# Delta-net stage of a two-layer trunk: a shorter key-norm chain, the first value pairs convolved from a copy, the inverse's placement rewritten

## The chip, the cores and the metric

The kernel runs on one core of a Trainium2 chip. A core has a matrix engine (PE, with its weight loads shown apart as PEld), and three elementwise engines: VectorE (DVE), ScalarE (ACT) and GpSimd (POOL). SyncE (SP) issues the DMAs. Each engine has its own queue of instructions, written out when the program is built, and waits in it on semaphores. The metric is device microseconds of one execution; lower is better. All times below are us unless another unit stands beside them.

## The reference

The input is one sequence of 256 tokens of width 1024. Two layers each add a half-weighted feed-forward block, a mixer and another half-weighted feed-forward block, each with an RMS norm ahead of it and behind it. The mixer of layer 0 is a gated short convolution. That of layer 1, where the change lies, is a gated delta rule:

```python
proj = x @ w_in                                  # q, k, v, z, b, a
qkv = silu(causal_depthwise_conv(qkv, conv_w))   # width 4
q, k = l2norm(q), l2norm(k)                      # 8 heads of 128, each used by 2 of 16 value heads
a = where(strict, (k_beta @ k.T) * decay, 0)     # per head and chunk of 64 tokens
t_inv = triangular_solve(eye + a, eye)
u, w = t_inv @ v_beta, t_inv @ (k_beta * exp(g))
# scan over chunks: v_new = u - w S; o = q_g S + qk v_new; S = S exp(g_last) + k_tail^T v_new
o = o * rsqrt(mean(o*o) + eps) * norm_w * silu(z)
out = o @ w_out
```

All of it is in float32.

## The kernel before

The 256 tokens are kept in SBUF. Tokens come in two tiles of 128 (index t, NT = 2). The weights are streamed: each piece of 512 KB is loaded to a buffer `raw` (3 buffers), split by ScalarE into a rounded part `whi` (L119) and by VectorE into the remainder `wlo` (L121); both have 8 buffers. Each product is then three matmuls, activation-high by weight-high, activation-low by weight-high and activation-high by weight-low. Most of the program is such products, back to back on PE.

The delta-net mixer (`gdn_proj`) issues its work in this order. Two head slabs give the gates and the first key and query heads. The tiles a0, a1, a2 (`stat_group`, L278 to L280, 24 matmuls of 256 columns for each head's part) give the other keys and queries; each is convolved (`conv`: one ScalarE instruction L584 and three on VectorE, L586) and passed through silu (L573). Three z groups follow, z0, z1 and z2 (`act_group`, L221, L222, L225: 24 matmuls of 512 columns for each of the two token tiles), then four value groups v0 to v3 (`stat_group` again, two pairs each), then z3, then the output product.

Beside these run chains that wait for their turn. `kq_chain` takes four groups of two key heads: PE transposes a head (L618) and forms the products of keys with keys and with queries (L621) in PSUM banks named `acc`; ScalarE copies the transposed key (`ktok`, L624) and part of the head (L625), and sums squares with four activations L630 into `kss`; POOL adds a small constant to all eight sums (L634), VectorE takes the reciprocal (L636), POOL multiplies it into `dsc` (L639), VectorE scales the products into `KQ` (L645, eight instructions), and ScalarE copies the eight 32-row diagonal blocks to `Ld` (L652). When all four groups are there, `invert` starts: VectorE transposes `Ld` (L669), then runs 31 steps of two dependent instructions (L677 multiplies, L679 subtracts) on all diagonal blocks at once, and transposes the result twice, to `Xd` (L681) and `Yd` (L683). POOL copies `Yd` into KQ. PE then forms products of 32 x 32 blocks in two halves: L707, whose `blk` operand is `Xd`, L718 and L719, and so on. `v_pair` convolves a pair of value heads straight from the PSUM bank, applies silu, transposes on PE (L757) and scales on ScalarE (L759). `scan` needs the inverse and the values.

Two things set the order. In the program, each chain is a generator that a ticker resumes: every few matmuls of a group are a tick, and `yield n` waits n ticks; INV_WAIT is the wait between the inverse's transposes and its products, V_WAIT that between a value pair's silu and its transposes. A scheduler then writes each engine's queue from this program by its own estimate of when operands are ready, so an instruction can stand earlier or later in the queue than in the program. Once built, a queue's order is fixed.

Of the kernel before, what the change touches and what calls it, by code (L numbers as in the profile page):

```python
# [7 lines left out]
F32 = mybir.dt.float32  # L8
F32R = mybir.dt.float32r
AF = mybir.ActivationFunctionType  # L10
ALU = mybir.AluOpType
PSUM = bass.MemoryType.PSUM

P = 128
T = 256
NT = 2
# [5 lines left out]
NG = 4  # L22
B32 = 32
EPS = 1e-6
# [6 lines left out]
NBIG = 8  # L31
NROW = 3
KQ_WAIT = 3
INV_WAIT = 37
V_WAIT = 4
SCAN_WAIT = 2
ORD = "00111222"
GORD = "00012222"
# [11 lines left out]
def trunk_kernel(ctx: ExitStack, tc: tile.TileContext, x, norm_g, w_gu, w_dn, sc_in, sc_cw, sc_out,  # L50
                 gdn_h0, gdn_h1, gdn_a0, gdn_a1, gdn_a2, gdn_v, gdn_z, gdn_cw, gdn_al, gdn_dt, gdn_nw, gdn_out, eye, upper, slower, out, stop=None):
    nc = tc.nc
    V, S, G, PE = nc.vector, nc.scalar, nc.gpsimd, nc.tensor
# [6 lines left out]
    sp = ctx.enter_context(tc.tile_pool(name="sp", bufs=2))  # L60
# [16 lines left out]
    phalf = const.tile([P, 4], F32, name="phalf")  # L77
# [49 lines left out]
    def slab(shape, dtype, name):  # L127
        return hp.tile(shape, dtype, name=name, tag="slab")
# [347 lines left out]
    def gdn_proj(xh, xl, mid):  # L476
# [102 lines left out]
        KQ = [[None] * NT for _ in range(NG)]  # L579
# [25 lines left out]
        def kq_chain():  # L605

            for gi in range(NG):
                ss = sp.tile([P, NT, 2, 2], F32, name="kss", bufs=2)
                k1 = slab([P, 2, 2, P], F32, "kq1")
                pkq = []  # L610
                for i in range(2):
                    kh = 2 * gi + i
                    while kq[kh] is None or tk.now < kq_time[kh] + KQ_WAIT:
                        yield 1
                    tp = side_bank().rearrange("p (t c) d -> p t c d", t=NT)
                    for t in range(NT):
                        for c in range(2):
                            PE.transpose(tp[:, t, c, :], kq[kh][:, c, t * P:(t + 1) * P], ident)  # L618
                    pk = side_bank().rearrange("p (t c) d -> p t c d", t=NT)
                    for t in range(NT):  # L620
                        PE.matmul(pk[:, t, :, :], lhsT=kq[kh][:, 0, t * P:(t + 1) * P],  # L621
                                  rhs=kq[kh][:, :, t * P:(t + 1) * P], start=True, stop=True)
                    pkq.append(pk)
                    S.activation(ktok[:, kh, :], tp[:, 0, 0, :], AF.Copy)  # L624
                    S.activation(k1[:, i, :, :], kq[kh][:, :, P:], AF.Copy)  # L625
                    kq1[kh] = k1[:, i, :, :]
                    for t in range(NT):
                        for c in range(2):
                            junk = sp.tile([P, 512], mybir.dt.bfloat16, name="junk", bufs=1)
                            S.activation(junk[:, 0:P], tp[:, t, c, :], AF.Square, accum_out=ss[:, t, c, i:i + 1])  # L630
                    yield 1
                while dec[1][gi] is None:
                    yield 1
                G.tensor_scalar(ss, ss, EPS, None, ALU.add)  # L634
                rk = sp.tile([P, NT, 2], F32, name="rk", bufs=2)
                V.reciprocal(rk, ss[:, :, 0, :])  # L636
                dd = small(f"dsc{gi}", 8).rearrange("p (t n) -> p t n", t=NT)
                for t in range(NT):
                    G.tensor_tensor(dd[:, t, :].rearrange("p (k v) -> p k v", k=2),  # L639
                                    beta[:, t, 4 * gi:4 * gi + 4].rearrange("p (k v) -> p k v", k=2),  # L640
                                    rk[:, t, :].unsqueeze(2).broadcast_to([P, 2, 2]), ALU.mult)
                for t in range(NT):
                    m = big([P, 4, 2, P], F32, "KQ")
                    for hv in range(4):
                        V.scalar_tensor_tensor(m[:, hv, :, :], pkq[hv // 2][:, t, :, :], dd[:, t, hv:hv + 1],  # L645
                                               bc(dec[t][gi][:, hv, :], 2), ALU.mult, ALU.mult)
                    KQ[gi][t] = m
                    for b in range(4):
                        r = slice(b * B32, (b + 1) * B32)
                        o = Ld[r, :, 8 * gi + t:8 * gi + t + 7:2].rearrange("p i v -> p v i")  # L650
                        i_ = m[r, :, 0, b * B32:(b + 1) * B32]
                        S.activation(o, i_, AF.Copy)  # L652
                n = small(f"nk{gi}", 4).rearrange("p (t n) -> p t n", t=NT)
                G.tensor_tensor(n, ss[:, :, 0, :], phalf.rearrange("p (t n) -> p t n", t=NT), ALU.pow)
                q = small(f"eq{gi}", 4).rearrange("p (t n) -> p t n", t=NT)
                G.tensor_scalar(q, ss[:, :, 1, :], 128.0 * EPS, None, ALU.mult)
                w = small(f"wt{gi}", 4)
                G.tensor_tensor(w, etail[:, 4 * gi:4 * gi + 4], dd[:, 0, :], ALU.mult)
                Dsc[gi], nk[gi], eq[gi], wt[gi] = dd, n, q, w
                yield 1  # L660
            tk.start(invert())


# [3 lines left out]
        def invert():  # L667
# [5 lines left out]
            for j in range(B32 - 1):  # L673
                n, m = B32 - 1 - j, j + 1
# [5 lines left out]
            Xd = row("blk").rearrange("p (a b) -> p a b", a=B32)  # L680
# [1 line left out]
            Yd = row("blk").rearrange("p (a b) -> p a b", a=B32)  # L682
            V.transpose(Yd.rearrange("p h i -> p i h"), X)  # L683
            T1 = row("blk").rearrange("p (a b) -> p a b", a=B32)
            for gi in range(NG):
                for t in range(NT):
                    for b in range(4):
                        r = slice(b * B32, (b + 1) * B32)
                        G.tensor_copy(KQ[gi][t][r, :, 0, r], Yd[r, 8 * gi + t:8 * gi + t + 7:2, :])
            yield INV_WAIT  # L690
            for half in range(2):
                hs = slice(16 * half, 16 * half + 16)
                gis = (2 * half, 2 * half + 1)
                E = {}
                for gi in gis:
                    E[gi] = slab([P, 8, 64], F32, "E64")
                    for b in range(2):
                        r = slice(b * B32, (b + 1) * B32)
                        G.tensor_copy(E[gi][r, :, r], Xd[r, 8 * gi:8 * gi + 8, :])
                    G.memset(E[gi][0:B32, :, B32:], 0.0)  # L700
                pt = side_bank().rearrange("p a (b c) -> p (a b) c", c=B32)
                for x in range(16):
                    ht = 16 * half + x
# [42 lines left out]
        nv = [None] * NG  # L746

        def v_pair(gi, i, pt, tiles):
            vc = sp.tile([P, 2, T], F32, name="yb")
            for j in range(2):  # L750
                conv(vc[:, j, :], pt[:, j, :], 16 + 4 * gi + 2 * i + j)
            silu(vc, vc)
            yield V_WAIT
            tp = ps.tile([P, NT, 2, P], F32, name="mm")
            for t in range(NT):
                for j in range(2):
                    PE.transpose(tp[:, t, j, :], vc[:, j, t * P:(t + 1) * P], ident)  # L757
            for t in range(NT):
                S.activation(tiles[t][:, 2 * i:2 * i + 2, :], tp[:, t, :, :], AF.Copy,  # L759
                             scale=nk[gi][:, t, i:i + 1])  # L760
            if i == 1:
                nv[gi] = tiles
# [293 lines left out]
```

## Time and profile before

| what | value |
|---|---|
| median of 3 runs | 1127.42 us (1125.82 to 1130.31) |
| profiled execution, own time | 1128.42 us |
| its span | 1126.5 us |
| mean granted PE clock | 0.995 |
| PE busy | 1100.2 us, 98% of the span |
| DVE, ACT, POOL busy | 749.9, 651.8, 88.8 us |
| HBM read | 195.99 MB |

The span is the time from the first to the last instruction of the profiled execution. PE's share is so high because nearly all of the program is matmuls in a row; where PE idles, it does so for single waits of a fraction of a microsecond to some microseconds. The delta-net stage lies at about 660 to 925 us of the span. In a timeline row, the number in square brackets is the engine's idle time ahead of the instruction and the instruction that ended it; the column after the start is the duration of the whole row.

### The profile page before, as it was taken

Reading aid. Unit: us, or ns where it says so; the run is one execution under the profiler, and the core shown is the slowest. Engines: PE = TensorE matmul, PEld = TensorE weight load, DVE = VectorE, ACT = ScalarE, POOL = GpSimd, SP = SyncE. Lnnn points to the kernel's source line nnn. Section 1 sums busy time; section 2 is a strip of 40 time slices with the busy share of each in tenths; the row PEclk is TensorE's granted clock in tenths of the full one; section 3 lists DMA queues with packets and bytes.
Section 4 is the critical chain, followed back from the end, with each engine's and each line's share of the span. In section 5 each row is a group of like instructions: output and inputs, shape, how many; then the busy total and the mean of one; then the engine's idle time right before and its main releaser. Section 6 shows DMA issues by size and latency. Waiting matters only on the chain.

```text
span 1126.5 us, 16842 instructions
## 1 busy us (share of the span) xinstructions
PE 1100.2 (98%) x6284; PEld 942.4 (84%) x6284; DVE 749.9 (67%) x1140; ACT 651.8 (58%) x1201; POOL 88.8 (8%) x167
## 2 busy tenths in 40 slices
PE   9999999999999999999999999889899999999997
PEld 6888887888788888788888877778899887888886
DVE  7776735687777663577765468768946557767543
ACT  6666535545556653556664358784587645666432
POOL 0100000000200000010000012110141212000000
PEclk9999999999999999999999999999999999999999
DMA  8755555656566565576555653327332355655552
GB/s 271 244 185 190 191 166 167 225 180 198 182 223 204 171 206 165 163 229 209 189 185 169 193 185 113 94 94 227 114 129 76 131 168 168 213 199 190 185 168 75
DMA packets 55955, 198.12 MB, mean 176 GB/s; under 512 B 6721, under 2 KB 7233, under 8 KB 55874
## 3 DMA queue, kind: packets, MB, share of 16 engines
q1 hardware_dynamic: 55728, 196.99, 54.2%
q8 instruction: 49, 0.80, 0.3%
q14 instruction: 32, 0.26, 0.1%
q10 hardware_dynamic: 146, 0.07, 0.0%
HBM read 195.99 MB, written 1.05 MB: 175 GB/s over the span
## 4 chain that ended last, share of the span: by engine, by line
PE 81%; DVE 7%; ACT 5%; DMA 3%; issue 2%; POOL 2%; SPq 0%; DVEq 0%; POOLq 0%; ACTq 0%
PE mm L298 27%; PE mm L301 14%; PE acc L324 7%; PE acc L325 7%; PE acc L323 7%; PE mm L221 3%; PE mm L222 3%; PE mm L225 3%; DVE wlo L121 2%; ACT whi L119 1%; ACT blk L652 1%; DVE kq L586 1%; PE mm L176 1%; ACT junk L147 1%; DMA raw<-in_w_gu 1%
## 5 line engine op out<-in xcount | busy, mean ns | idle before, releaser
L121 DVE TENSOR_TENSOR wlo<-raw,whi 128x1024 fp32r<-128x1024 f32 (+2 forms) x362 | 437.5, 1220 | 240.2 <-ACT whi L119 201.5
L119 ACT ACTIVATE whi<-raw 128x1024 fp32r<-128x1024 f32 (+2 forms) x362 | 376.1, 1051 | 224.3 <-PE acc L325 104.6
L298 PE MATMUL mm<-x,whi 128*128 128x512 f32 x1312 | 329.4, 393 | 0.0
L298 PEld LDWEIGHTS mm<-x,whi 128*128 128x128 f32 x1312 | 235.9, 189 | 42.4
L301 PEld LDWEIGHTS mm<-x,wlo 128*128 128x128 f32 x1312 | 179.0, 190 | 12.8
L301 PE MATMUL mm<-x,wlo 128*128 128x256 f32 x1312 | 182.9, 282 | 0.0
L323 PE MATMUL acc<-whi,hb 128*128 128x512 f32 x352 | 136.5, 388 | 0.0
L324 PE MATMUL acc<-wlo,hb 128*128 128x512 f32 x352 | 135.6, 385 | 0.3 <-DVE wlo L121 0.3
L325 PE MATMUL acc<-whi,hb 128*128 128x512 f32 x352 | 135.3, 385 | 0.0
L308 ACT ACTIVATE corr<-mm 128x256 f32<-128x256 f32 x164 | 61.2, 376 | 67.4 <-PE mm L301 65.6
L221 PE MATMUL mm<-whi,x 128*128 128x512 f32 (+1 forms) x240 | 94.4, 394 | 0.9 <-ACT x L178 0.7
L222 PE MATMUL mm<-wlo,x 128*128 128x512 f32 (+1 forms) x240 | 94.2, 393 | 0.7 <-DVE wlo L121 0.7
L225 PE MATMUL mm<-whi,x 128*128 128x512 f32 (+1 forms) x240 | 87.8, 389 | 0.2 <-DVE x L179 0.2
L324 PEld LDWEIGHTS acc<-wlo,hb 128*128 128x128 f32 x352 | 66.2, 188 | 13.8 <-DVE wlo L121 0.8
L323 PEld LDWEIGHTS acc<-whi,hb 128*128 128x128 f32 x352 | 66.2, 188 | 13.1
L325 PEld LDWEIGHTS acc<-whi,hb 128*128 128x128 f32 x352 | 66.1, 188 | 13.2
L154 POOL TENSOR_SCALAR rstd<-ss 128x1 f32<-128x1 f32 x24 | 12.3, 513 | 786.1 <-ACT junk L147 786.1
L278 PE MATMUL mm<-x,whi 128*128 128x256 f32 x200 | 59.7, 299 | 2.0 <-DVE kq L586 2.0
L279 PE MATMUL mm<-x,whi 128*128 128x256 f32 x200 | 58.4, 292 | 0.0
L280 PE MATMUL mm<-x,wlo 128*128 128x256 f32 x200 | 57.9, 289 | 0.0
L222 PEld LDWEIGHTS mm<-wlo,x 128*128 128x128 f32 x240 | 45.2, 188 | 11.2 <-DVE wlo L121 2.9
L221 PEld LDWEIGHTS mm<-whi,x 128*128 128x128 f32 x240 | 45.2, 188 | 11.1 <-ACT x L178 2.7
(216 smaller groups left out, 1238.3 us busy)
## 6 DMA issues: line engine op xcount, KB each, us to landing
raw<-in_w_gu SPq DMA_DIRECT2D x176, 512.0 KB, 4.2
raw<-in_w_dn SPq DMA_DIRECT2D x88, 512.0 KB, 3.6
raw<-in_sc_in SPq DMA_DIRECT2D x24, 512.0 KB, 4.1
raw<-in_gdn_z SPq DMA_DIRECT2D x16, 512.0 KB, 3.9
raw<-in_gdn_v SPq DMA_DIRECT2D x16, 512.0 KB, 4.2
raw<-in_gdn_out SPq DMA_DIRECT2D x16, 512.0 KB, 3.7
gamma<-in_norm_g SPq DMA_DIRECT2D x11, 512.0 KB, 5.4
raw<-in_gdn_a SPq DMA_DIRECT2D x9, 512.0 KB, 4.4
```

The costliest lines, as they stand in the source:

```text
L119: S.activation(hi[:, r], raw[:, r], AF.Copy)
L121: newest[0] = V.tensor_tensor(lo[:, r], raw[:, r], hi[:, r], ALU.subtract).ins
L221: PE.matmul(pt, lhsT=xh[:, t, k, :], rhs=hi, start=(k == 0), stop=False)
L222: PE.matmul(pt, lhsT=xh[:, t, k, :], rhs=lo, start=False, stop=False)
L225: PE.matmul(pt, lhsT=xl[:, t, j, :], rhs=part(j)[0], start=False, stop=(j == KD - 1))
L278: PE.matmul(ptile, lhsT=hi, rhs=h2, start=(k == 0), stop=False)
L298: PE.matmul(flat, lhsT=part(k, 0), rhs=xx[:, k].rearrange("p h t q -> p (h t q)"), start=(k == 0), stop=False)
L301: PE.matmul(flat[:, T:], lhsT=part(k, 1), rhs=xx[:, k, 0].rearrange("p t q -> p (t q)"), start=False, stop=(k == KD - 1))
L308: S.activation(c, pt[:, 1, :], AF.Copy)
L323: PE.matmul(o, lhsT=yh(c, t), rhs=hi[:, r], start=(c == 0), stop=False)
L324: PE.matmul(o, lhsT=yh(c, t), rhs=lo[:, r], start=False, stop=False)
L325: i = PE.matmul(o, lhsT=yl(c, t), rhs=hi[:, r], start=False, stop=(c == n - 1)).ins
```

## The change

In the key-norm chain, `kss` is laid out with the keys' sums first. The squares come ahead of the copies of `ktok` and of the head, and the key's two ahead of the query's two. The addition of the constant and the two `dsc` products go from POOL to VectorE, the addition for the four key sums alone; POOL adds the constant for the queries' sums where it scales them. Of the eight block copies of a group (four for each token tile), the four of rows 64 to 127 go from ScalarE to POOL. In `invert`, the fills of `E` and the copies of the diagonal blocks are written as a function, called for the first half of the heads ahead of the wait and for the second half behind it, with POOL's order fixed among them; the wait is 41 ticks where it was 37. In `v_pair`, the pairs of v0 and v1 are first copied by ScalarE from their PSUM bank to a slab buffer `vraw` and convolved from there; the wait ahead of their transposes is 8 ticks where it was 4, and 4 for v2 and v3 as before. Behind the change the lines of `gdn_proj` have other numbers: L618 becomes L619, L645 L646, L669 L673, L677 and L679 become L681 and L683, L681 and L683 become L685 and L687, L707 becomes L724, L711 L728, L757 L778.

```diff
-INV_WAIT = 37
-V_WAIT = 4
+INV_WAIT = 41
+V_WAIT = (8, 8, 4, 4)
+VRAW = 2
...
-                ss = sp.tile([P, NT, 2, 2], F32, name="kss", bufs=2)
+                ss = sp.tile([P, 2, NT, 2], F32, name="kss", bufs=2)
...
+                    for c in range(2):
+                        for t in range(NT):
+                            junk = sp.tile([P, 512], mybir.dt.bfloat16, name="junk", bufs=1)
+                            S.activation(junk[:, 0:P], tp[:, t, c, :], AF.Square, accum_out=ss[:, c, t, i:i + 1])
                     S.activation(ktok[:, kh, :], tp[:, 0, 0, :], AF.Copy)
                     S.activation(k1[:, i, :, :], kq[kh][:, :, P:], AF.Copy)
                     kq1[kh] = k1[:, i, :, :]
-                    for t in range(NT):
-                        for c in range(2):
-                            junk = sp.tile([P, 512], mybir.dt.bfloat16, name="junk", bufs=1)
-                            S.activation(junk[:, 0:P], tp[:, t, c, :], AF.Square, accum_out=ss[:, t, c, i:i + 1])
...
-                G.tensor_scalar(ss, ss, EPS, None, ALU.add)
+                V.tensor_scalar(ss[:, 0], ss[:, 0], EPS, None, ALU.add)
                 rk = sp.tile([P, NT, 2], F32, name="rk", bufs=2)
-                V.reciprocal(rk, ss[:, :, 0, :])
+                V.reciprocal(rk, ss[:, 0])
                 dd = small(f"dsc{gi}", 8).rearrange("p (t n) -> p t n", t=NT)
                 for t in range(NT):
-                    G.tensor_tensor(dd[:, t, :].rearrange("p (k v) -> p k v", k=2),
+                    V.tensor_tensor(dd[:, t, :].rearrange("p (k v) -> p k v", k=2),
...
-                        S.activation(o, i_, AF.Copy)
+                        if b < 2:
+                            S.activation(o, i_, AF.Copy)
+                        else:
+                            G.tensor_copy(o, i_)
...
+            E, placed = {}, [None]
+
+            def place(half):
+
+                gis = (2 * half, 2 * half + 1)
+                for gi in gis:
+                    E[gi] = slab([P, 8, 64], F32, "E64")
+                    for b in range(2):
+                        r = slice(b * B32, (b + 1) * B32)
+                        with tc.issue_after(placed[0]) if placed[0] else nullcontext():
+                            G.tensor_copy(E[gi][r, :, r], Xd[r, 8 * gi:8 * gi + 8, :])
+                    with tc.issue_after(placed[0]) if placed[0] else nullcontext():
+                        last = G.memset(E[gi][0:B32, :, B32:], 0.0).ins
+                placed[0] = last
...
+            place(0)
             yield INV_WAIT
             for half in range(2):
...
+                if half:
+                    place(1)
                 pt = side_bank().rearrange("p a (b c) -> p (a b) c", c=B32)
...
+            if gi < VRAW:
+                raw = slab([P, 2, T], F32, "vraw")
+                S.activation(raw, pt, AF.Copy)
+                pt = raw
...
-            yield V_WAIT
+            yield V_WAIT[gi]
```

What this does to the queues is seen at three places. The first is PE's queue around the inverse's first products (`blk` is Xd; a number behind a name tells buffers apart). Before, they stand among the matmuls of v2's first pair (bank 7875), behind the transposes of three value pairs:

```order
L757 MATMUL mm_7888<-ident_81,yb_7803 128x128 x2
...
L280 MATMUL mm_7875<-x2_5783,wlo_7852 128x256
L278 MATMUL mm_7875<-x2_5783,whi_7857 128x256
L279 MATMUL mm_7875<-x2_5783,whi_7857 128x256
L280 MATMUL mm_7875<-x2_5783,wlo_7858 128x256
L707 MATMUL acc_7937<-blk_7350,KQ_6831 32x32
L707 MATMUL acc_7937<-blk_7350,KQ_6840 32x32 x2
```

After the change they stand between z2's first token tile (bank 7495) and its second (bank 7522), ahead of every value group (v0's first bank is 7575):

```order
L223 MATMUL mm_7495<-wlo_7492,x2_5783 128x512
L226 MATMUL mm_7495<-whi_7491,x2_5783 128x512
L724 MATMUL acc_7988<-blk_7350,KQ_6831 32x32
L724 MATMUL acc_7988<-blk_7350,KQ_6840 32x32 x2
...
L222 MATMUL mm_7522<-whi_7473,x2_5783 128x512
L223 MATMUL mm_7522<-wlo_7474,x2_5783 128x512
...
L279 MATMUL mm_7575<-x2_5783,whi_7551 128x256
```

So the products moved ahead past z2's second tile, all of v0 and v1 and a part of v2's first pair. The second place is VectorE's queue in the steps of the inverse. Before, convolutions (L586) and weight remainders (L121) stand among the steps up to the last one:

```order
L677 TENSOR_TENSOR sg<-blk 128x247
L586 SCALAR_TENSOR_TENSOR yb<-mm,gcw,yb 128x255
L679 TENSOR_TENSOR blk<-blk,sg 128x13x19
L586 SCALAR_TENSOR_TENSOR yb<-mm,gcw,yb 128x254
L677 TENSOR_TENSOR sg<-blk 128x240
L586 SCALAR_TENSOR_TENSOR yb<-mm,gcw,yb 128x253
L679 TENSOR_TENSOR blk<-blk,sg 128x12x20
```

After the change the last weight remainder (L122) among them is that of v0's fourth piece; from the subtraction over 22 x 10 on, 43 instructions of the steps follow in a row up to the two transposes, and v1's remainders and the first convolutions (now L587, from `vraw`) come behind:

```order
L681 TENSOR_TENSOR sg<-blk 128x220
L122 TENSOR_TENSOR wlo<-raw,whi 128x1024
L683 TENSOR_TENSOR blk<-blk,sg 128x22x10
L681 TENSOR_TENSOR sg<-blk 128x231
...
L683 TENSOR_TENSOR blk<-blk,sg 128x31
L685 STREAM_TRANSPOSE blk<-blk 128x32x32
L687 STREAM_TRANSPOSE blk<-blk 128x32x32
L122 TENSOR_TENSOR wlo<-raw,whi 128x1024 x4
L587 SCALAR_TENSOR_TENSOR yb<-vraw,gcw,yb 128x255 x2
```

The third place is VectorE's queue at the last key-norm group. Before:

```order
L121 TENSOR_TENSOR wlo<-raw,whi 128x1024 x3
L636 RECIPROCAL rk<-kss 128x4
L645 SCALAR_TENSOR_TENSOR KQ<-acc,dsc_7210,dec 128x256 x8
L121 TENSOR_TENSOR wlo<-raw,whi 128x1024
L669 STREAM_TRANSPOSE blk<-blk 128x1024
```

After:

```order
L122 TENSOR_TENSOR wlo<-raw,whi 128x1024 x2
L635 TENSOR_SCALAR kss<-kss 128x4
L122 TENSOR_TENSOR wlo<-raw,whi 128x1024
L637 RECIPROCAL rk<-kss 128x4
L640 TENSOR_TENSOR dsc_7210<-beta,rk 128x4 x2
L646 SCALAR_TENSOR_TENSOR KQ<-acc,dsc_7210,dec 128x256 x8
L122 TENSOR_TENSOR wlo<-raw,whi 128x1024
L673 STREAM_TRANSPOSE blk<-blk 128x1024
```

The addition and the two products are now in VectorE's own queue, in front of the eight scalings.

More of the change, by code (lines that the diff above doesn't have):

```diff
@@ L651, in kq_chain @@
                         i_ = m[r, :, 0, b * B32:(b + 1) * B32]
-                        S.activation(o, i_, AF.Copy)
+                        if b < 2:
+                            S.activation(o, i_, AF.Copy)
+                        else:
+                            G.tensor_copy(o, i_)
                 n = small(f"nk{gi}", 4).rearrange("p (t n) -> p t n", t=NT)
-                G.tensor_tensor(n, ss[:, :, 0, :], phalf.rearrange("p (t n) -> p t n", t=NT), ALU.pow)
+                G.tensor_tensor(n, ss[:, 0], phalf.rearrange("p (t n) -> p t n", t=NT), ALU.pow)
                 q = small(f"eq{gi}", 4).rearrange("p (t n) -> p t n", t=NT)
-                G.tensor_scalar(q, ss[:, :, 1, :], 128.0 * EPS, None, ALU.mult)
+                G.tensor_scalar(q, ss[:, 1], EPS, 128.0 * EPS, ALU.add, ALU.mult)
                 w = small(f"wt{gi}", 4)
@@ L684, in invert @@
             T1 = row("blk").rearrange("p (a b) -> p a b", a=B32)
-            for gi in range(NG):
-                for t in range(NT):
-                    for b in range(4):
-                        r = slice(b * B32, (b + 1) * B32)
-                        G.tensor_copy(KQ[gi][t][r, :, 0, r], Yd[r, 8 * gi + t:8 * gi + t + 7:2, :])
+            E, placed = {}, [None]
[4 more added lines that the diff above has]
+                    for b in range(2):
+                        r = slice(b * B32, (b + 1) * B32)
+                        with tc.issue_after(placed[0]) if placed[0] else nullcontext():
[3 more added lines that the diff above has]
+                placed[0] = last
+                for gi in gis:
+                    for t in range(NT):
+                        for b in range(4):
+                            r = slice(b * B32, (b + 1) * B32)
+                            with tc.issue_after(placed[0]):
+                                last = G.tensor_copy(KQ[gi][t][r, :, 0, r], Yd[r, 8 * gi + t:8 * gi + t + 7:2, :]).ins
+                placed[0] = last
+            place(0)
             yield INV_WAIT
@@ L693, in invert @@
                 gis = (2 * half, 2 * half + 1)
[L694 to L700, printed above, removed]
+                if half:
+                    place(1)
                 pt = side_bank().rearrange("p a (b c) -> p (a b) c", c=B32)
```

## The prediction

> **What bounds the kernel now.** I read the page's busy times first, then PE's waits in the delta-net stage, then the timelines around each wait. The page:
>
> ```profile
> PE 1100.2 (98%) x6284; PEld 942.4 (84%) x6284; DVE 749.9 (67%) x1140; ACT 651.8 (58%) x1201; POOL 88.8 (8%) x167
> ```
>
> PE is the bound nearly everywhere, so an edit on another engine is worth what it takes away from, or adds to, PE's idle time. All the change's instructions lie in the delta-net stage. PE's waits there, 640 to 940 us (us in total, times, longest):
>
> ```profile
> PE acc L618 <- ACT kq L573: 3.6, 2, 3.1
> PE mm L757 <- ACT yb L573: 3.4, 1, 3.4
> PE mm L278 <- DVE kq L586: 2.0, 1, 2.0
> PE acc L621 <- DVE KQ L645: 1.7, 1, 1.7
> PE acc L718 <- ACT blk L711: 0.4, 1, 0.4
> PE acc L707 <- DVE blk L681: 0.2, 1, 0.2
> ```
>
> These six make 11.3 us, most of what any reordering here could win. The last row matters: the inverse's first products wait 0.2 us for Xd, so before the change they stand at just the right place. PE's timeline gives each wait's place and what follows it:
>
> ```profile
> 732.18 1.13 PE L621 MATMUL acc<-kq 128*128 128x256 f32 x4 [1.71 <-DVE KQ L645]
> 746.69 1.12 PE L618 MATMUL acc<-ident,kq 128*128 128x128 f32 x4 [3.06 <-ACT kq L573]
> 750.09 0.39 PE L221 MATMUL mm<-whi,x 128*128 128x512 f32 x1
> 767.13 0.39 PE L221 MATMUL mm<-whi,x 128*128 128x512 f32 x1
> 772.57 0.39 PE L221 MATMUL mm<-whi,x 128*128 128x512 f32 x1
> 778.01 0.28 PE L278 MATMUL mm<-x,whi 128*128 128x256 f32 x1
> 794.53 1.12 PE L757 MATMUL mm<-ident,yb 128*128 128x128 f32 x4 [3.41 <-ACT yb L573]
> 795.65 0.41 PE L279 MATMUL mm<-x,whi 128*128 128x256 f32 x1
> 797.57 0.37 PE L279 MATMUL mm<-x,whi 128*128 128x256 f32 x1
> 797.90 0.28 PE L278 MATMUL mm<-x,whi 128*128 128x256 f32 x1
> 798.02 0.28 PE L279 MATMUL mm<-x,whi 128*128 128x256 f32 x1
> ```
>
> z1's second tile ends at 767.13, z2's first runs from there to 772.57 (5.44 us), z2's second to 778.01. Behind the 3.41 us wait the clock is low: nine steps take 797.57 - 795.65 = 1.92 us, 0.213 each, where one takes 0.12 (797.90 to 798.02). With the four transposes this loses 1.5 us. Behind the 3.06 us wait the same count (746.69 to 750.09 is 3.40 us for about 1.4 us of work at full clock) gives 2.0 us. The granted clock in the slices of 10 us (start:end, length, PE, PEld, DVE, ACT, POOL, then the clock) agrees:
>
> ```profile
> 740.00:750.00 10.00, 6.94 (x26) 5.48 (x25) 6.08 (x11) 8.55 (x30) 0.25 (x2) 0.83 0.36 110
> 790.00:800.00 10.00, 6.59 (x44) 6.39 (x43) 9.97 (x26) 6.57 (x10) 0.00 (x0) 0.83 0.22 63
> ```
>
> A page of the Trainium skill, "TensorE: Matmul & The Clock Gate" (Part 1, What's actually happening), says the clock is halved after an idle window of about 3.4 us; by it every wait of that length costs some 1.7 us more (an estimate: half of one such window), as the two slices of this trace show. The sum stands on the 1.5 and 2.0.
>
> **The key-norm part: a gain of 6.5 us on PE.** The last group's chain across ACT, POOL and DVE:
>
> ```profile
> 744.43 1.04 ACT L119 ACTIVATE whi<-raw 128x1024 fp32r<-128x1024 f32 x1
> 746.02 0.62 ACT L573 ACTIVATE kq<-kq 128x512 f32<-128x512 f32 x1
> 748.81 0.28 ACT L630 ACTIVATE junk<-acc 128x128 bf16<-128x128 f32 x1
> 749.67 0.24 POOL L634 TENSOR_SCALAR kss<-kss 128x8 f32<-128x8 f32 x1 [12.43 <-ACT junk L630]
> 749.94 0.18 DVE L636 RECIPROCAL rk<-kss 128x4 f32<-128x4 f32 x1 [2.43 <-POOL kss L634]
> 751.65 3.23 DVE L645 SCALAR_TENSOR_TENSOR KQ<-acc,dsc,dec 128x256 f32<-128x256 f32 x8 [1.53 <-POOL dsc L639]
> 753.34 1.85 ACT L652 ACTIVATE blk<-KQ 32x128 f32<-32x128 f32 x4 [0.82 <-DVE KQ L645]
> 756.18 1.80 ACT L652 ACTIVATE blk<-KQ 32x128 f32<-32x128 f32 x4
> 758.02 1.25 DVE L669 STREAM_TRANSPOSE blk<-blk 128x1024 f32<-128x1024 f32 x1 [2.01 <-ACT blk L652]
> ```
>
> From the sums' end (749.67) to the first scaling (751.65) the chain takes 2.0 us through POOL and back. In VectorE's queue the addition, the reciprocal and two products are four small instructions, 0.1 to 0.2 each by the 0.18 row, with one weight remainder between them: 1.6, so 0.4 won in the last group and 1.4 in one with no remainder between. The key's squares are done two squares (0.8) sooner. Half the block copies leave ACT: 1.85 becomes 0.9, while POOL, 8% busy, does the rest in the same time. ACT so frees about 0.9 per tile ahead of each silu and weight split, and the silu at 746.02 that PE waited for comes some 3 us earlier. Following each queue in its new order from 707 us on with durations from such rows, I get the last group's sums at 744.7 (before 749.6) and the chain's transpose at 751.1 (before 758.0). On PE the waits of 3.06 and 1.71 and the 2.0 of low clock go, 6.8, and a little is given back where a product waits for the copy of `ktok`, which now stands behind four squares: 0.3. So z1 ends at 767.13 - 6.5 = 760.6, z2's first tile at 766.0. Bounds: nothing (the VectorE queue now holds what POOL did, and a late square would stop its remainders and convolutions too), and 7.3, all of the four rows' L618 and L621 waits with the clock, without L278's 2.0, whose predecessors are the same.
>
> **The moved products: the term that decides.** PE's queue now holds the first products between z2's two tiles. They need Xd, and VectorE's queue holds ahead of Xd eight weight remainders, among them v0's four, and the whole chain:
>
> ```profile
> 760.40 1.21 DVE L121 TENSOR_TENSOR wlo<-raw,whi 128x1024 fp32r<-128x1024 f32 x1
> 761.53 0.20 DVE L679 TENSOR_TENSOR blk<-blk,sg 128x31 f32<-128x31 f32 x1
> 773.68 0.39 DVE L679 TENSOR_TENSOR blk<-blk,sg 128x220 f32<-128x220 f32 x1
> 788.07 0.42 DVE L677 TENSOR_TENSOR sg<-blk 128x252 f32<-128x252 f32 x1
> 788.53 0.42 DVE L679 TENSOR_TENSOR blk<-blk,sg 128x252 f32<-128x252 f32 x1
> 809.80 2.20 DVE L681 STREAM_TRANSPOSE blk<-blk 128x1024 f32<-128x1024 f32 x1
> 811.89 1.96 DVE L683 STREAM_TRANSPOSE blk<-blk 128x1024 f32<-128x1024 f32 x1
> ```
>
> The 43 instructions from the one over 220 elements to the end run with nothing between. Busy time of L677 and of L679 in that stretch:
>
> ```profile
> 773.60:809.60 36.00, 7.47 (x22) 0.95 0.52 157
> 773.60:809.60 36.00, 7.80 (x22) 0.95 0.52 157
> ```
>
> That is 15.3, and a dependent pair is 0.46 apart where each lasts 0.42 (788.07, 788.53), 0.04 more for each of 43: 17.0. The transpose adds 2.1 (809.80 to 811.89): 19.1. Ahead of the 43 stand the first transpose (1.2), 19 smaller instructions (about 5.4 from 0.19 up to 0.38) and eight remainders of 1.13 (760.40 to 761.53): 15.7, and about 0.9 of waiting for a weight split, so from 751.1 they begin at 767.7 and Xd is there at 786.8. PE has come to the products at 766.0: it waits **20.8 us**.
>
> A lower bound needs no start of the chain. The last of v0's remainders needs its weight split, and that one needs a buffer that z1's last matmul frees. So Xd is at least 1.04 + 1.13 + 19.1 = 21.3 behind z1's end, and PE has only z2's first tile, 5.4, to do in that time: a wait of at least 15.9, whatever the key-norm part wins. Before, the z2 tile, v0 and v1 stood ahead of the products, and this was their cover.
>
> z2's second tile then starts at 786.8 where it started at 772.57: +14.2 (the products themselves are paid in both). The low clock behind such a wait, by the two losses above: +1.8, between 1.5 and 2.0; a longer wait may not lower it for longer, but no row shows one.
>
> **The values.** The pairs of v0 and v1 cost one copy each on ACT, bounded by the silu of the same 128 x 512 (0.62) and the weight split (1.04); four of them are 2.5 to 4.2 us of ACT work, hidden by PE's products as ACT is 58% busy, and if that cover went, each would hold a transpose by its 0.6 to 1.0. What held the transposes at 794.53 was that convolutions stood among the chain's steps and remainders in VectorE's queue. Now the chain is done before v0 begins, and the transposes come four ticks later, so the wait and its low clock go: 3.41 + 1.5 = 4.9. The 0.4 and 0.2 at L718 and L707 go or come back in the same size: -0.3. Behind the products I find nothing new that waits: the blocks' fills on POOL for the first half run beside z2's second tile and v0. Two norm loads stand two weight loads later on SP's queue; DMA is under half busy there (share 0.22 in the slice at 790).
>
> **The sum.** +14.2 + 1.8 - 4.9 - 0.3 = +10.8; the 6.5 is already in the 14.2. Against the profiled execution that is a span of 1126.5 + 10.8 = 1137.3 and a time of 1128.42 + 10.8 = 1139.2. That execution lies 1.0 above the median shown, so the median becomes 1127.42 + 10.8 = **1138**. Below 0.5%, 5.6 us, a change can't be told from none here.
>
> **Rivals.** *The key-norm part wins more.* If the chain starts at 745 instead of 751, the buffer for v0's split sets the end, and the wait is its bound: Xd at 760.6 + 21.3 = 781.9, 9.3 late: 9.3 + 1.8 - 5.2 = +5.9, 1133. For it: POOL waited 12.43 us for the last squares. Against: those wait for PE's own transposes.
>
> *The key-norm part wins nothing.* VectorE now waits in its queue for ACT's squares, the remainders behind it come late, and the chain starts at 758 as before. From there Xd takes 35.7 (786.8 - 751.1): 793.7, 21.1 late: 21.1 + 1.8 - 5.2 = +17.7, 1145. For it: the reciprocal's wait of 2.43 already stands in front of remainders. Against: the silu and the squares have fewer copies ahead of them on ACT.
>
> *PE passes the waiting products.* If PE could start z2's second tile while the 32 x 32 products wait, nothing of the 20.8 is seen, and the gains add up: 6.5 + 4.9 + 0.3 = 11.7, a time of 1116, faster. It decides from the point where a ready matmul stands behind a waiting one. Against: at 794.53 PE idled 3.41 us at the transposes, and the matmuls behind them use weights of a group that was already being multiplied; none started. The Trainium skill's page "TensorE: Matmul & The Clock Gate" (Part 3, The mechanism) says that matmuls start and end in program order; the trace's 3.41 agrees.
>
> *A smaller wait.* All PE waits before z2 go, L278's 2.0 and its low clock too, and the wait is at its bound of 15.9: the +5.9 less 3.8 (2.0 and some 1.8 of low clock) is about +2, 1130, no change that can be told. That needs the convolution at 707 to come sooner, which nothing in the change moves.
>
> **Chances.** The forecast holds 0.60, the larger gain 0.13, no gain 0.15, the small wait 0.07, the passing 0.05. The forecast's own range is 1134 to 1142. The larger gain lies at the edge of what can be told, 1133.1, so I give half of it to no change: slower 0.60 + 0.15 + 0.07 = 0.82, same 0.13, faster 0.05. The range of 8 in 10 goes from 1130 to 1146.
>
> **What will show it.** A single wait of PE at the inverse's first products for the transpose Xd, 16 to 21 us between z2's tiles, and one slice with PE nearly empty and a low clock near 770 to 790; the wait of 3.4 at the value transposes gone; VectorE's transpose of `Ld` near 751 (758 or later: the key-norm part wins nothing); four small instructions on VectorE in place of the wait for POOL's `kss`. The prediction is wrong if that wait is under 10 us, or if PE is seen to multiply z2's second tile inside it.

## The result and the profile after

The changed kernel takes 1139.92 us (median of 4, 1139.72 to 1142.22) where the kernel before takes 1128.87 on the same scale (median of 4); the ratio is 1.0104 with a 95% interval of 1.0074 to 1.0134, some 8 to 15 us slower. The prediction was 1138, a difference of 10.8 where 11.1 was measured. The profiled execution has a span of 1138.4, 11.9 above that of before.

PE's waits in the delta-net stage of the changed kernel (us in total, times, longest):

```profile
PE acc L724 <- DVE blk L685: 21.5, 1, 21.5
PE mm L279 <- DVE kq L587: 2.0, 1, 2.0
PE mm L177 <- DVE xs L169: 1.3, 2, 0.7
PE acc L622 <- ACT ktok L629: 1.0, 1, 1.0
```

The three waits of before that the change aimed at (3.6 and 1.7 in the key-norm stage, 3.4 at the value transposes) are gone. One stands in their place, at the inverse's first products, and it is longer than all of them. PE's timeline shows where: the end of z2's first tile, the products, z2's second tile, and the first matmul of v0.

```profile
765.67 0.39 PE L226 MATMUL mm<-whi,x 128*128 128x512 f32 x1
787.60 1.92 PE L724 MATMUL acc<-blk,KQ 32*32 32x32 f32 x64 [21.54 <-DVE blk L685]
789.45 0.80 PE L222 MATMUL mm<-whi,x 128*128 128x512 f32 x1
793.45 0.47 PE L222 MATMUL mm<-whi,x 128*128 128x512 f32 x1
796.96 0.28 PE L279 MATMUL mm<-x,whi 128*128 128x256 f32 x1
```

VectorE's timeline shows what PE waits for: the last group's sums and scalings, the chain's first transpose, the last weight remainder among the steps, the first of the 43 instructions, and Xd.

```profile
744.38 0.17 DVE L635 TENSOR_SCALAR kss<-kss 128x4 f32<-128x4 f32 x1 [1.04 <-ACT junk L628]
746.09 3.23 DVE L646 SCALAR_TENSOR_TENSOR KQ<-acc,dsc,dec 128x256 f32<-128x256 f32 x8
751.24 1.25 DVE L673 STREAM_TRANSPOSE blk<-blk 128x1024 f32<-128x1024 f32 x1 [0.79 <-POOL blk L656]
767.34 1.23 DVE L122 TENSOR_TENSOR wlo<-raw,whi 128x1024 fp32r<-128x1024 f32 x1
768.48 0.38 DVE L683 TENSOR_TENSOR blk<-blk,sg 128x220 f32<-128x220 f32 x1
785.52 2.03 DVE L685 STREAM_TRANSPOSE blk<-blk 128x1024 f32<-128x1024 f32 x1
```

Xd is there at 787.55, where before it came at 812.0: Xd is 24 us earlier, and the kernel is slower, because PE comes to fetch it 46 us earlier: at 766.0, where before it came at 811.9. In the slices of 10 us (PE busy first, granted clock behind POOL) there is one with nothing on PE:

```profile
760.00:770.00 10.00, 6.06 (x27) 4.69 (x25) 8.50 (x16) 5.67 (x8) 0.00 (x0) 0.99 0.74 236
770.00:780.00 10.00, 0.00 (x0) 0.00 (x0) 9.25 (x23) 0.00 (x0) 0.00 (x0) 0.50 0.14 49
780.00:790.00 10.00, 2.40 (x65) 2.29 (x66) 8.67 (x20) 0.39 (x1) 2.14 (x6) 0.50 0.00 0
790.00:800.00 10.00, 10.00 (x50) 8.57 (x49) 4.13 (x4) 5.63 (x7) 6.28 (x16) 0.82 0.37 101
```

ScalarE, POOL and the DMA stand nearly still too: ScalarE waits 20.4 us for the products' results (L728), POOL 35.2 for Xd itself (the fills of `E`, L699), and the loads up to 25.8 for weight remainders that stand behind the steps in VectorE's queue.

One caution when the two traces are laid side by side. The first matmul of the a tiles starts at 687.35 before and at 689.40 after, and nothing of the change runs ahead of it, so 2.05 of the 11.9 are a difference between executions. Below, "from the stage's start" means from these two instants; by that clock the change costs 9.9 in this pair of profiles, within the interval of the timed runs.

### The profile page after: what moved, and what is told of

It is laid out like the page before. It is cut to its first block, busy times and chain, and to the rows that moved or that the text cites. A ratio compares the mean times of both kernels' runs of the same rounds, so it can differ in the third digit from the quotient of the medians.

```text
span 1138.4 us, 16880 instructions
## 1 busy us (share of the span) xinstructions
PE 1099.2 (97%) x6284; PEld 941.9 (83%) x6284; DVE 753.6 (66%) x1152; ACT 646.2 (57%) x1189; POOL 96.5 (8%) x171
## 3 DMA queue, kind: packets, MB, share of 16 engines
HBM read 195.99 MB, written 1.05 MB: 173 GB/s over the span
## 5 line engine op out<-in xcount | busy, mean ns | idle before, releaser
L122 DVE TENSOR_TENSOR wlo<-raw,whi 128x1024 fp32r<-128x1024 f32 (+2 forms) x362 | 436.5, 1218 | 248.3 <-ACT whi L120 208.0
L222 PE MATMUL mm<-whi,x 128*128 128x512 f32 (+1 forms) x240 | 96.8, 403 | 1.4 <-ACT x L179 1.3
L226 PE MATMUL mm<-whi,x 128*128 128x512 f32 (+1 forms) x240 | 89.0, 393 | 0.0
L279 PE MATMUL mm<-x,whi 128*128 128x256 f32 x200 | 58.2, 291 | 2.0 <-DVE kq L587 2.0
L280 PE MATMUL mm<-x,whi 128*128 128x256 f32 x200 | 57.3, 287 | 0.0
L223 PEld LDWEIGHTS mm<-wlo,x 128*128 128x128 f32 x240 | 45.9, 191 | 10.8 <-DVE wlo L122 2.2
```

Of the source, the lines that this page charges most:

```text
L122: newest[0] = V.tensor_tensor(lo[:, r], raw[:, r], hi[:, r], ALU.subtract).ins
L222: PE.matmul(pt, lhsT=xh[:, t, k, :], rhs=hi, start=(k == 0), stop=False)
L223: PE.matmul(pt, lhsT=xh[:, t, k, :], rhs=lo, start=False, stop=False)
L226: PE.matmul(pt, lhsT=xl[:, t, j, :], rhs=part(j)[0], start=False, stop=(j == KD - 1))
L279: PE.matmul(ptile, lhsT=hi, rhs=h2, start=(k == 0), stop=False)
L280: PE.matmul(ptile, lhsT=hi, rhs=l2, start=False, stop=False)
```

## The experiments

Theory A says that the loss is the place of the products in PE's queue, that the rewritten placement puts them there, and that the other two parts of the change gain. Theory B puts the loss on the key-norm part, theory C on the copies of the values, theory D on the early fills and the unbroken run of the chain. All ratios are against the kernel before, run on the same chip in the same job; 1% is 11.3 us.

| run | what it is | median us | ratio, 95% interval |
|---|---|---|---|
| 1 | placement alone | 1149.64 | 1.0173, 1.0154 to 1.0191 |
| 2 | key-norm part alone | 1120.93 | 0.9922, 0.9900 to 0.9943 |
| 3 | values alone | 1131.13 | 1.0008, 0.9993 to 1.0022 |
| 4 | the change, E late | 1123.41 | 0.9948, 0.9930 to 0.9966 |
| 5 | the change, products pinned | 1136.69 | 1.0045, 1.0028 to 1.0061 |
| 6 | the change without the values | 1141.64 | 1.0098, 1.0083 to 1.0113 |
| 7 | 2 with all blocks on ScalarE | 1128.59 | 0.9982, 0.9971 to 0.9993 |
| 8 | 2 with later v0 transposes | 1120.68 | 0.9912, 0.9896 to 0.9929 |
| 9 | 2 with 3 of 4 blocks on POOL | 1117.39 | 0.9883, 0.9865 to 0.9901 |
| 10 | 2 and values, waits 6 and 37 | 1121.82 | 0.9914, 0.9892 to 0.9935 |
| 11 | 2 with all blocks on POOL | 1119.99 | 0.9912, 0.9889 to 0.9934 |
| 12 | 9 with later v0 transposes | 1119.53 | 0.9902, 0.9882 to 0.9922 |

**Run 1, the placement alone.** The kernel before with the hunk of the change in `invert`, the wait left at 37:

```diff
-            for gi in range(NG):
-                ... (all copies of Yd into KQ)
+            E, placed = {}, [None]
+            def place(half): ...
+            place(0)
             yield INV_WAIT
             for half in range(2):
-                E = {} ... (allocated and filled here)
+                if half:
+                    place(1)
```

> The kernel before with nothing but the inverse's placement rewritten (E of the first half allocated and filled ahead of the wait, the rest of the copies by halves); the wait is 37 ticks as before, the key-norm chain and the values are as before. Its queues: PE has the first products between z2's two tiles, VectorE has nine weight remainders among the steps and nothing between the last ones. Theory A (the loss is the place of the products, and this rewriting brings it): the chain starts at 758 as before, Xd comes 36 to 37 us later at about 794, PE waits 21 to 22 us for it between z2's tiles; with 2 us of low clock and without the 4.9 us at the value transposes the time is about 17 to 20 us above the kernel before, 1145 to 1148. Theory B (the key-norm part on VectorE and POOL costs the time): within 3 us of the kernel before.

It lost 19.5 us, with one new wait and all the old ones of the key-norm stage:

```profile
PE acc L721 <- DVE blk L682: 23.4, 1, 23.4
PE acc L619 <- ACT kq L574: 3.6, 2, 3.1
PE acc L622 <- DVE KQ L646: 1.7, 1, 1.7
```

Nothing of the key-norm part is in this kernel, so B falls and A stands; its number, 17 to 20, held too. (The wait is 23.4 where A had 21 to 22.)

**Run 2, the key-norm part alone.** The kernel before with the hunk of the change in `kq_chain`.

> The kernel before with the key-norm part alone (order of the squares, additions and products on VectorE, half of the block copies on POOL). PE's first products stand in v2's first pair as before. Theory A: PE's waits of 3.1 and 1.7 us in the key-norm stage and the low clock behind them are gone, z1 ends 6 to 9 us earlier, the wait of 3.4 at the value transposes stays or shrinks: 5 to 9 us below the kernel before, 1119 to 1124. Theory B: slower than before by 2 us or more.

9 us faster, at the upper end of what A said. Both waits in the key-norm stage are gone, and the one at the value transposes has shrunk from 3.4, since the chain begins sooner, its first transpose at 63.1 from the stage's start where it was at 70.7 before, and ends sooner:

```profile
PE mm L765 <- ACT yb L574: 2.1, 2, 1.8
PE mm L279 <- DVE kq L587: 2.0, 1, 2.0
```

**Run 3, the values alone.** The kernel before with the hunk in `v_pair`, `VRAW = 2` and `V_WAIT = (8, 8, 4, 4)`.

> The kernel before with the value part alone (pairs of v0 and v1 copied to a buffer by ScalarE, waits of 8 ticks ahead of their transposes). Theory A: the wait of 3.4 us at the value transposes and its low clock go: 3 to 5 us below the kernel before. Theory C (the copies load ScalarE and so cost): slower than before by 1 us or more, with PE waiting for ScalarE in the value groups.

No gain that can be told, and no loss: C falls, and so does A's number. The wait at the transposes is gone as A had it, but another stands behind it:

```profile
PE acc L708 <- DVE blk L682: 4.2, 1, 4.2
PE acc L619 <- ACT kq L574: 2.6, 1, 2.6
```

PE skips the wait for the convolutions and so arrives that much sooner at the products, and Xd has not come any sooner: VectorE has the same work ahead of it, and the transpose to Xd begins 122.4 from the stage's start here and 122.5 before. The wait was moved, not removed.

**Run 4, the change with E late.** One line moved:

```diff
-            place(0)
             yield INV_WAIT
+            place(0)
```

> The changed kernel whole, with one line moved: the first half's placement is called behind the wait of 41 ticks and not ahead of it. PE's first products then stand in v3's first pair, and weight remainders and convolutions stand among the inverse's steps again. Theory A: no wait at the first products, the key-norm and the value gains both seen: 9 to 12 us below the kernel before, 1116 to 1120. Theories B and C: 1128 or more.

The 21.5 us are gone and the kernel is 6 us faster than before, some 17 us faster than the change (16.5 by the medians, 17.6 by the two ratios, 1.0104 less 0.9948): the line's place decides the sign. (In its queue the products stand in v2's second pair, not in v3's first as the expectation has it.) It is less than A's 9 to 12, and by its ratio less than run 2, though the two intervals overlap; a later value transpose now waits, behind the chain's last transposes on VectorE:

```profile
PE mm L778 <- ACT yb L574: 2.7, 1, 2.7
```

How a line that only fills a buffer moves matmuls: E is taken from the slab pool and written ahead of the wait, and the scheduler then lists the products ahead of z2's second tile. The line also issues the first half's copies of `Yd` into KQ, but these stand ahead of the wait in the kernel before too, with the products in v2's first pair; built with only these copies ahead of the wait, the changed kernel has the products in v2's second pair, and built with only E ahead of it, between z2's tiles (neither was run). The longer wait that the change writes has no hold on it: run 1 has 37 ticks and the products in the same place, and so has the changed kernel when it is built with 37, 45 or 53 (not run). Why the scheduler does so, no run shows.

**Run 5, the change with the products pinned.** E stays early; the first products are ordered behind the last value matmul issued before them.

```diff
-            PE.matmul(ptile, lhsT=lo, rhs=h2, start=False, stop=(k == KD - 1))
+            lastmm[0] = PE.matmul(ptile, lhsT=lo, rhs=h2, start=False, stop=(k == KD - 1)).ins
...
+                        with tc.issue_after(lastmm[0]):
                             PE.matmul(pt[r1, x, :], lhsT=m[r0, (ht // 2) % 4, 0, r1], rhs=Xd[r0, ht, :],
```

> The changed kernel whole, with E still early, and with the first products ordered on PE behind the last value matmul that the program has issued ahead of them. VectorE's queue is that of the changed kernel (43 instructions of the chain in a row, then v1's remainders); only PE's queue differs: z2's second tile, v0, v1 and a part of v2 stand ahead of the products again. Theory A (PE's queue order is what turns Xd's time into idle PE): the 21.5 us wait is gone; PE runs z2 and v0 to about 783 and then waits 6 to 8 us for v1's first remainder, which comes behind the chain at about 790; with the low clock this is 13 to 16 us below the changed kernel, 2 to 5 below the kernel before. Theory D (the early fills and copies themselves, or VectorE's long run of the chain, hold PE, and the order on PE matters little): no more than 5 us below the changed kernel.

It lies between: about 7 us below the change (1.0104 less 1.0045), not 13 to 16, and still above the kernel before. The wait for Xd is gone, and what A named in its place came: PE waits 5.1 for v1's first remainder, where A had 6 to 8, and 0.9 for a later one. Others came with it.

```profile
PE mm L282 <- DVE wlo L122: 6.0, 2, 5.1
PE acc L737 <- ACT blk L730: 2.6, 1, 2.6
PE mm L223 <- ACT zs L575: 1.9, 1, 1.9
PE acc L803 <- DVE rsol L849: 1.1, 1, 1.1
```

So the order on PE makes the one long wait, and VectorE's 43 instructions without a weight remainder between them make a part of the loss of their own: v1's remainders come behind the chain, and PE waits for those instead. D has that much right. The early E brings both: of the 17 us between the change and run 4, PE's order mended alone takes away 7, and some 11 remain (1.0045 less 0.9948).

**Run 6, the change without the values.** `VRAW = 0`, `V_WAIT = (4, 4, 4, 4)`, the rest as changed.

> The changed kernel without the value part (v0 and v1 convolved from their banks, waits of 4 ticks). Theory A as it was written (the value part and the later transposes remove the 4.9 us at the value transposes): 3 to 5 us above the changed kernel. Theory A2 (in the changed kernel the chain is over before v0 begins, so nothing stands among the convolutions and the wait goes without the value part): within 1.5 us of the changed kernel, 9 to 13 above the kernel before.

1.0098 against the change's 1.0104: A2. The value part is worth nothing that can be told in the changed kernel, and the wait at the transposes is all but gone without it:

```profile
PE acc L724 <- DVE blk L685: 21.2, 1, 21.2
PE mm L778 <- ACT yb L574: 0.6, 2, 0.4
```

**Run 7, the key-norm part with all blocks on ScalarE.** Against run 2:

```diff
-                        if b < 2:
-                            S.activation(o, i_, AF.Copy)
-                        else:
-                            G.tensor_copy(o, i_)
+                        S.activation(o, i_, AF.Copy)
```

> The key-norm part alone, as in the second run, but with all block copies on ScalarE as in the kernel before, so that only the squares' order and the move of the small instructions to VectorE are left of it. If the gain of 9 us comes mostly through the shorter way from the sums to the scalings: 6 to 9 us below the kernel before. If it comes mostly through the ScalarE time that half of the block copies free: 1 to 4 us below it.

Only 2 us below the kernel before. Of the 9 us of run 2, some 7 come from the ScalarE time that the block copies free, and not from the shorter way between sums and scalings. The page's row of PE's longest wait and ScalarE's row show it: the silu that PE waits for is as late as it was, 58.7 from the stage's start in both, behind four block copies and a weight split.

```profile
PE acc L619 <- ACT kq L574: 3.5, 1, 3.5
```

```profile
744.72 1.71 ACT L653 ACTIVATE blk<-KQ 32x128 f32<-32x128 f32 x4
747.40 0.63 ACT L574 ACTIVATE kq<-kq 128x512 f32<-128x512 f32 x1
```

**Run 8, later transposes on top of run 2.** `V_WAIT = (6, 4, 4, 4)`.

> The key-norm part alone, with a wait of 6 ticks and not 4 ahead of v0's transposes. In the run of the key-norm part alone PE still waits 1.8 us at v0's first transposes and 0.3 at the next; the first lies 24 matmuls or 2.9 us later here, so both go: 1 to 2 us below the key-norm part alone, if nothing else comes to wait.

Not told apart from run 2 (0.9912 and 0.9922, with intervals that overlap). The profile shows 1.3 us left at the transposes and 0.8 each at L711 and L722 of the inverse, where run 2 had nothing and 0.3. Again the wait moved.

**Runs 9 and 11, more blocks on POOL.** `if b < 1` in the place of `if b < 2`; then all copies as `G.tensor_copy`.

> The key-norm part alone with three of four block copies on POOL, one on ScalarE. If what it gains is ScalarE's freed time (the seventh run gained little with none on POOL, the second 9 us with half), the other key-norm waits are already gone with half, and so little is left: within 2 us of the key-norm part alone. If POOL's copies held up by VectorE's remainders (0.88 us for two, 1.82 where a remainder runs) come to set the start of the inverse, the chain starts 1 to 2 us later, which PE does not see, as the products have no wait in that run.

> The key-norm part alone with all block copies on POOL and none on ScalarE. With none, half and three quarters on POOL the kernel was 2, 9 and 13 us below the kernel before. If ScalarE's freed time is all that counts: 13 to 16 us below. If POOL's copies now bound the chain's start (in the run with three quarters the chain's transpose already waits 1.2 us for POOL): the chain starts 1 to 2 us later than there, and since the products have no wait for Xd in that run, 11 to 13 us below.

With three quarters on POOL the kernel is 12 to 13 us faster than before, the fastest here. That is some 4 us below run 2, where the expectation had at most 2, but the two intervals meet at 0.990. With all on POOL it is 10 us faster, nearer to the second forecast than to the first; the intervals of runs 9 and 11 overlap, so these two are not told apart. The chain's transpose waits longer for POOL as more copies go there, 0.79 with half, then:

```profile
750.15 1.25 DVE L673 STREAM_TRANSPOSE blk<-blk 128x1024 f32<-128x1024 f32 x1 [1.23 <-POOL blk L656]
```

```profile
750.14 1.25 DVE L670 STREAM_TRANSPOSE blk<-blk 128x1024 f32<-128x1024 f32 x1 [2.16 <-POOL blk L653]
```

so a part of what ScalarE wins POOL may give back. From the stage's start (689.34 and 688.51) the chain begins at 60.8 and 61.6. Run 2, with half, has it at 63.1 (750.87 less 687.78), but in that execution the clock was low behind the 2.0 us wait near 708 (0.94 and 0.89 in the slices from 700 to 720), and in runs 9 and 11 it was full; run 10, with half and a full clock, has 61.7. PE's largest wait is that of the value transposes in both, 2.5 us in run 9 and 4.2 in run 11. The profiled spans of runs 2, 9, 11 and 12 are 1116.9 to 1117.9, so the medians' difference between runs 2 and 9 rests on the timed runs alone.

**Runs 10 and 12, the values or later transposes on top.** Run 10 has the key-norm part, the copies of v0 and v1 and `V_WAIT = (6, 6, 4, 4)`, E late; run 12 is run 9 with `V_WAIT = (6, 4, 4, 4)`.

> The key-norm part and the value part, E late as in the kernel before, with waits of 6 ticks ahead of the first four transposes and 37 ahead of the products. The run with 8 and 41 ticks lost 2.5 us against the key-norm part alone, with a wait of 2.7 us at a later value transpose. If that wait is due to the place of the transposes: the time falls to that of the key-norm part alone or 1 us below. If the value part only shifts the wait, as where it stood alone: again 1 to 4 us above the key-norm part alone, with a wait at the products for Xd or at another transpose.

> Three quarters of the block copies on POOL, and a wait of 6 ticks and not 4 ahead of v0's transposes. The run with three quarters still shows a wait of 2.5 us at the value transposes. Later transposes take it away, or it comes back as a wait for Xd at the products, as in the runs where the value part stood without the early E: between 0 and 3 us below the run with three quarters, so 1114 to 1118.

Neither gains on what it was added to by more than can be told. Run 12 was expected 0 to 3 us below run 9 and is 2 us above it, within the intervals. Run 10 has the time of the first forecast (0.9914 against run 2's 0.9922) and the wait of the second, so it settles neither; the wait is at the products again:

```profile
PE acc L711 <- DVE blk L685: 3.3, 1, 3.3
```

With the three runs before (3, 4, 8) that makes five in which the value transposes were helped and the time did not fall by an amount that can be told. In runs 3, 8, 10 and 12 PE then waits for Xd or for ScalarE's copies behind it, in run 4 at a later value transpose.

## Why the prediction was right, and where not

**What bounds it, and the moved products.** The step on which the sign hung was that the products stand between z2's tiles and that VectorE has 15.7 + 19.1 us to do between the chain's start and Xd. Predicted: chain's transpose 751.1, the 43 from 767.7, Xd 786.8, z2's first tile done 766.0, wait 20.8. Measured: 751.24, 768.48, 787.55, about 766.0, 21.54. Runs 1 and 4 show that the placement causes it. The wait did not fall to its lower bound of 15.9, which lets v0's last weight split begin at z1's end: z1 ended at 760.46, and that split began at 766.25, when its load had come.

**Partly luck in the absolute times.** The stage began 2.05 later in the profile after. From the stage's start, z2's first tile began at 71.1 (760.46 less 689.40) where it began at 79.8 before: a gain of 8.7 on PE, where the sum had 6.5. Some 1.4 to 1.8 of the difference is a low clock behind the 2.0 us wait at 707.5, seen before (granted clock 0.95 and 0.88 in the slices from 700 to 720, 1.7 us of lost clock) and not after (1.00 and 1.00), with the same wait in both. It differs from execution to execution: of the fourteen that were profiled eight have it and six have not. With the same key-norm part PE begins v0 at 83.2 from the stage's start where the clock was low (run 2) and at 81.8 where it was full (run 10). With the low clock in both, run 2 against the kernel before, PE begins v0 7.5 sooner (at 83.2 and not 90.7), near the 6.5 of the sum. The wait at the products came out as predicted since two errors nearly cancel: from the stage's start PE came to the products 2.0 sooner than forecast and Xd 1.3 sooner. The 0.3 given back at the copy of `ktok` was 1.0, the row L622 above.

**The rest of the sum.** From the stage's start:

| term | predicted | measured |
|---|---|---|
| Xd against the old start of z2's second tile | +14.2 | 98.2 - 85.2 = +13.0 |
| low clock behind the wait | +1.8 | 2.07 on z2's tile and 0.72 on the products: +2.8 |
| wait and clock at the value transposes | -4.9 | -4.9: the wait is gone, its price is that of the rows before |
| L718, L707 and small ones | -0.3 | -1.0: not measured, the rest of the difference |
| sum | +10.8 | +9.9 |

z2's second tile took 796.96 - 789.45 = 7.51 where 5.44 was usual, and the products 1.85 where they take 1.13 at full clock before. The clock term was sized from waits of 3 us; the low clock behind 21.5 us lasted from 787.60 to 793.45, 5.9 us, where behind the 3.41 us wait it was about 3 (794.53 to 797.57).

**The step that was wrong in its cause.** "Now the chain is done before v0 begins, and the transposes come four ticks later, so the wait and its low clock go: 4.9." The size held, and the first half of the sentence; the second half and the value part had no share. Run 6 keeps the gain without them, and where E is late the value part (runs 3, 4 and 10) or later transposes alone (runs 8 and 12) earn nothing that can be told, in most of them because PE comes sooner to products that are no sooner ready. Read as what the value part alone is worth, the -4.9 would be nothing (run 3: 1.0008).

**The key-norm part.** The sum gave it 6.5 at z1's end; alone it is worth 9 us over the whole kernel (run 2, 6 to 11 by its interval). The two are not the same thing: the 9 holds what the earlier chain takes off the wait at the value transposes too (3.4 to 2.1, and its low clock), which the sum had under the values. The step's parts were weighed wrongly: the shorter way from the sums to the scalings, which the text worked out first, brings 2 us together with the squares' order (run 7), the freed ScalarE time 7. That VectorE would be held by waits for squares, the rival of no gain, does not show: the wait in front of L635 is 1.04 and that of L636 was 2.43.

**The rivals.** No pass of the waiting products: z2's second tile, whose weights had been in use for the first tile, stood still for 21.5 us. For most of that it was ready: in run 5, where nothing stands in its way, it starts at 768.9, when a silu of an earlier z group has freed its bank. The Trainium skill's "TensorE: Matmul & The Clock Gate" (Part 3, The mechanism), that matmuls start and end in program order, agrees with PE's row at 787.60. The rival of the larger gain had its chain start at 745 and saw 751; the small wait needed L278's wait gone, which is there unchanged (2.0).

## What to carry to other kernels

Where queues are fixed at build time, an instruction that waits long blocks all that stands behind it (PE for 21.5 us here), so look in the queue for the consumer of a long chain and count the work ahead of it against what its producer has yet to do: here 5.4 us against 21.3, which settled the sign without any timing of the new code. A wait that is taken away ahead of a later one, with the later one's producer unchanged, comes back there, as runs 3 and 10 show most plainly; ask first which chain ends last. And a change in three parts can hold a gain of 9 us (run 2) behind a loss of 20 (run 1), so it pays to time the parts apart.

## What had not been expected of the hardware

A POOL instruction that starts while VectorE runs a weight remainder (128 x 1024, both sources in SBUF) takes about a microsecond longer and ends 0.05 to 0.9 us behind the remainder's end, while the remainder keeps its 1.2 us. In the changed kernel, the same small POOL instruction beside a remainder and beside a scaling that reads PSUM, and the power instruction in the same two places:

```profile
732.32 1.24 POOL L660 TENSOR_SCALAR eq<-kss 128x4 f32<-128x4 f32 x1 [2.19 <-DVE kq L587]
746.66 0.19 POOL L660 TENSOR_SCALAR eq<-kss 128x4 f32<-128x4 f32 x1
744.69 1.88 POOL L658 TENSOR_TENSOR nk<-kss,phalf 128x4 f32<-128x4 f32 x1 [4.27 <-DVE kss L635]
715.18 1.04 POOL L658 TENSOR_TENSOR nk<-kss,phalf 128x4 f32<-128x4 f32 x1 [9.62 <-DVE kss L635]
749.38 1.82 POOL L656 COPY blk<-KQ 32x128 f32<-32x128 f32 x2 [0.62 <-DVE KQ L646]
747.88 0.88 POOL L656 COPY blk<-KQ 32x128 f32<-32x128 f32 x2 [0.75 <-DVE KQ L646]
```

```profile
732.29 1.22 DVE L122 TENSOR_TENSOR wlo<-raw,whi 128x1024 fp32r<-128x1024 f32 x1
744.48 1.23 DVE L122 TENSOR_TENSOR wlo<-raw,whi 128x1024 fp32r<-128x1024 f32 x1
749.24 1.22 DVE L122 TENSOR_TENSOR wlo<-raw,whi 128x1024 fp32r<-128x1024 f32 x1
```

The pair of block copies at 749.38 is the one that the chain's transpose waits 0.79 us for. In the kernel before, a power instruction that began just ahead of a remainder (727.61 and 727.66) took its usual 1.05, and the remainder its 1.23. That the two engines share their way to SBUF, as the Trainium skill's "GPSIMD Engine Reference" (1. Specifications) says, agrees with these rows; no run here separates it from other causes.
